# The output projection of a gated streaming-encoder block: seven products of halves in place of eight

## The chip, the cores and the metric

The kernel runs on one core of a Trainium2 chip. The metric is the device time of one execution in microseconds (us); the figure for a kernel is the median of its runs. A profile is one execution of its own, with its own time. PE is the matrix engine (TensorE), DVE VectorE, ACT ScalarE, POOL GpSimd, SP the engine that issues most of the DMAs.

## The reference, cut to what matters

One layer for 2048 tokens of width 1024, all in f32. The normalised input goes through one wide projection; branch A is banded attention, branch B ("ret") retention with a per-head norm; each branch is gated and projected back to width 1024; the two are mixed, projected once more, added to the input and normalised:

```python
branch_a = jnp.einsum('bsf,fd->bsd', o_a * jax.nn.silu(g_a), w_out_attn[l])
branch_r = jnp.einsum('bsf,fd->bsd', o_r * jax.nn.silu(g_r), w_out_ret[l])
mixed = jax.nn.sigmoid(m_a) * branch_a + jax.nn.sigmoid(m_r) * branch_r
x = x + jnp.einsum('bsd,de->bse', mixed, w_out[l]).astype(x.dtype)
...
return rms_norm(x, final_gain)
```

The change is in the line with `w_out`: a product of (2048 x 1024) by (1024 x 1024), and in how its operands are made.

## The kernel before, in words

**Products.** Every f32 matrix is kept as a high part (a cast to fp32r, on ACT) and a low part (source minus high part, on DVE or POOL). A "product" multiplies a stationary block of 512 x 128 by a moving block of 512 x 512: four slices `k` of 128, each with three matmuls of 128x512 (high by high, high by low, low by high), so 12 matmuls (`Chunk.matmuls`). The moving block lies in one of seven resident slots `R[0]` to `R[6]`, each with a high and a low tile. The stationary block is made by `make`: one ACT cast (L296) and one subtraction (L297).

**Jobs and steps.** The work on PE is one list of products, `seq`, in the order of the jobs: `p0`, `g0`, `p1`, `g1` (the wide projection), `ba0`, `ba1` (branch A's output), `br0`, `br1` (branch B's output), `out`. A job has chunks, a chunk has products. `dense()` walks the list; a product takes four steps, and `later(n, f)` runs `f` n steps on. `prime(at + ahead + 1)` with `AHEAD = 3` makes the stationary block of a product three products before PE comes to it.

**Two kinds of chunks.** `Plain` chunks (`ba`, `br`, `out`) multiply halves the ordinary way: for 256 output columns or tokens, two column halves `c`, two row halves `i` and two inner halves `j`, so eight products a chunk. `Strassen` chunks (`p`, `g`) form sums of halves and need seven: `SUMS_OF` gives four sums t1 to t4 of the streamed operand, made on POOL; the resident operand needs the quarter blocks A11, A12, A22 and four sums, in slots as `PRODUCTS` numbers them; `Strassen.product` combines the seven results with one ACT copy (`u2`) and five DVE additions, and calls `epilogue` four times. `ORDERS` are the orders in which the seven are done. The products' results lie in the PSUM banks "x", "y", "v", "z", "w", all from the pool `ACC` (4 banks); in the last phase another pool, `TR` (4 banks), stands open.

**The last phase** (`mrg`) holds the end of `g1`, the branch projections and `out`. There `strict[0]` is False: ACT, DVE and POOL instructions may be ordered by the framework rather than by the program; PE and the SP queue stay in program order. Row blocks of branch outputs are loaded into slots by `fill_ya`, `fill_yr` and `finish_yr`, at places given by `RYA` and `RYR`. All these small 128x512 buffers come from one pool `E` of 23 (`E_MRG`). `out` streams the mixed rows (`raw_out`, two loads of 512 KB a chunk, SP queue, three buffers) as stationary blocks; its four moving blocks are the quarters of `w_out`, loaded, cast and subtracted into slots 0, 2, 3, 4 by `fill_wo` (L1130) from hooks in `br1`. In `br`, each output half needs two operand loads (`gr`, `ta`), one DVE operation (L1124), one POOL addition (L1125) and a store.

**The output's epilogue** (`ep_out`, L1156). `before_out` loads 128x512 of x (`xr`) and of the final gain (`fg`). When a pair of products is done, DVE forms xr = 0.25 ps + xr (L1161), ACT squares it with a row sum (L1166), POOL multiplies by the gain (L1167). When both halves of a 128-token row are there, DVE computes the reciprocal root in tiny 128x1 operations (L1172, then `rsqrt`, L196 to L204), and the halves are scaled, one on ACT (L1175), one on DVE (L1174), and stored six steps later. The last row's first half is stored from ACT's queue.

Of the kernel before, what the change touches and what calls it, by code (L numbers as in the profile page):

```python
# [21 lines left out]
P = 128  # L22
# [23 lines left out]
ORDERS["f"] = LAST = (0, 3, 1, 2, 4, 5, 6)  # L46
AHEAD = 3
# [23 lines left out]
def hybrid_kernel(  # L71
# [196 lines left out]
    class Chunk:  # L268
# [42 lines left out]
        def bank(self, name):  # L311
            if name not in self.ps:
                self.ps[name] = ACC(f"ps_{self.job.name}_{self.c}_{name}")
            return self.ps[name]
# [13 lines left out]
    class Strassen(Chunk):  # L328
        def sum(self, dst, one, two, ring=None):
            b = self.b  # L330
            if dst in b:
                return
            name = f"{dst}_{self.job.name}_{self.c}"
            t = wp.tile([P, 4, P], F32, tag="t", bufs=SUMS, name=name) if ring is None else \
                ring(name).rearrange("p (k c) -> p k c", k=4)
            b[dst] = self.shaped(t)
            pool.tensor_tensor(b[dst], b[one], b[two], ALU.subtract)

# [75 lines left out]
    class Job:  # L414
        def __init__(self, name, n, stream, epilogue, lo_pool=(), kh=2, resident=None, before=None, front=0):
# [10 lines left out]
            if name == "p1":  # L426
                self.orders[:2] = "first", "second"
            seq = [(c, k) for c in range(front, n) for k in (per if resident else ORDERS[self.orders[c]])]
# [22 lines left out]
    def dense(jobs):  # L451
# [14 lines left out]
        sooner[at - 9], sooner[at - 6] = (one, [0]), (one, [1])  # L466
        for at, (job, ch, n) in enumerate(seq):
# [9 lines left out]
            while starts and starts[0] <= at + job.lead:  # L477
                _, ch2, n2 = seq[starts.pop(0)]
                ch2.before(n2)
            for _ in ch.product(n):  # L480
# [649 lines left out]
    def fill_wo(i, j, m):  # L1130
        def fetch(k):
            a = E(f"wo_{i}_{j}_{k}")
            row = (4 * j + k) * P
            dma(a, w_out[0, row:row + P, 512 * i:512 * i + 512])
            later(10, lambda: act.copy(R[m][0][:, k, :], a))
            later(12, lambda: dve.tensor_tensor(R[m][1][:, k, :], a, r32(R[m][0][:, k, :]), ALU.subtract))

        for k in range(4):
            later(1 + 2 * k, lambda k=k: fetch(k))
# [16 lines left out]
    def ep_out(c, i, j, src, got):  # L1156

        t = 2 * c + j
        xr, fg = got

        dve.scalar_tensor_tensor(xr, src, 0.25, xr, ALU.mult, ALU.add)  # L1161
        if t not in rows_out:
            rows_out[t] = ({}, small.tile([P, 2], F32, tag="fs", bufs=4, name=f"fs_{t}"))
        halves_, fs = rows_out[t]
        junk = E(f"jk_{t}_{i}", BF16)
        act.activation(junk, xr, AF.Square, scale=DM ** -0.5, accum_out=fs[:, i:i + 1])  # L1166
        pool.tensor_tensor(fg, xr, fg, ALU.mult)  # L1167
        halves_[i] = fg
        if len(halves_) < 2:
            return  # L1170
        ft, fr, tm, hv = (small.tile([P, 1], F32, tag=f"f{n}", bufs=2, name=f"f{n}_{t}") for n in range(4))
        dve.scalar_tensor_tensor(ft, fs[:, 0:1], NORM_EPS, fs[:, 1:2], ALU.add, ALU.add)  # L1172
        rsqrt(ft, fr, tm, hv)
        dve.tensor_scalar(halves_[1], halves_[1], fr, None, ALU.mult)  # L1174
        act.mul(halves_[0], halves_[0], fr)  # L1175
        for f in range(2):
            dst = out[0, t * P:(t + 1) * P, 512 * f:512 * f + 512]
            if t == SEQ // P - 1 and not f:
                act.dma_start(dst, halves_[f])
            else:  # L1180
                put(6, dst, halves_[f])
# [444 lines left out]
    RYA = [{(0, 0): 0, (1, 0): 4}, {(0, 0): 6, (1, 0): 1}]  # L1626
    RYR = [{(0, 0): 5, (0, 1): 3, (1, 0): 2, (1, 1): 0}, {(0, 0): 4, (0, 1): 6, (1, 0): 1, (1, 1): 5}]
    RWO = {(0, 0): 0, (0, 1): 2, (1, 0): 3, (1, 1): 4}
# [6 lines left out]
    jobs.append(Job("out", 8, mx_stream, ep_out, resident=RWO, before=before_out))  # L1635
# [14 lines left out]
    for i in range(2):  # L1650
        hook("ba0", 1 + i, 0, lambda i=i: fill_ya(1, i, RYA[1][i, 0]))
        hook("br1", 1 + i, 0, lambda i=i: fill_wo(i, 1 - i, RWO[i, 1 - i]))
    hook("br1", 0, 0, lambda: fill_wo(0, 0, RWO[0, 0]))
    hook("br1", 3, 4, lambda: fill_wo(1, 1, RWO[1, 1]))

# [146 lines left out]
```

## Time and profile before

| what | value |
|---|---|
| median of 3 runs | 1987.76 us (1986.89 to 1991.05) |
| profiled execution, its own time | 1993.2 us |
| its span, first to last instruction | 1991.4 us |
| mean granted TensorE clock | 0.996 |
| PE busy | 1926.9 us (97%) |
| DVE, ACT, POOL busy | 1353.9 (68%), 911.1 (46%), 898.8 us (45%) |
| DMA | 434.85 MB, mean 218 GB/s |

Busy shares are means over stages that differ: what a change in `out` is worth is read from the last 175 us of the span alone.

### The profile page before, as it was taken

Reading aid. Unit: us, or ns where it says so; the run is one execution under the profiler, and the core shown is the slowest. Engines: PE = TensorE matmul, PEld = TensorE weight load, DVE = VectorE, ACT = ScalarE, POOL = GpSimd, SP = SyncE. Lnnn points to the kernel's source line nnn. Section 1 sums busy time; section 2 is a strip of 40 time slices with the busy share of each in tenths; the row PEclk is TensorE's granted clock in tenths of the full one; section 3 lists DMA queues with packets and bytes.
Section 4 is the critical chain, followed back from the end, with each engine's and each line's share of the span. In section 5 each row is a group of like instructions: output and inputs, shape, how many; then the busy total and the mean of one; then the engine's idle time right before and its main releaser. Section 6 shows DMA issues by size and latency. Waiting matters only on the chain.

```text
span 1991.4 us, 30303 instructions
## 1 busy us (share of the span) xinstructions
PE 1926.9 (97%) x9712; PEld 1604.3 (81%) x9712; DVE 1353.9 (68%) x2585; ACT 911.1 (46%) x1835; POOL 898.8 (45%) x735
## 2 busy tenths in 40 slices
PE   6899999999999999999999999999999999999998
PEld 4777778888888877778787888888888878888886
DVE  7887878677766658888887677765566655544554
ACT  6454454566654545443333555554455221222332
POOL 2343544555546665544544444454675114422222
PEclk9999999999999999999999999999999999999999
DMA  4576695756549987676675645554989999976564
GB/s 148 162 258 198 217 309 197 211 153 181 159 135 276 276 248 258 192 242 195 193 247 177 185 148 177 155 147 141 281 268 294 319 334 338 326 251 213 187 200 138
DMA packets 335054, 434.85 MB, mean 218 GB/s; under 512 B 30040, under 2 KB 194544, under 8 KB 334896
## 3 DMA queue, kind: packets, MB, share of 16 engines
q1 hardware_dynamic: 277744, 377.07, 59.6%
q10 hardware_dynamic: 57152, 55.85, 9.3%
q8 instruction: 78, 1.28, 0.3%
q14 instruction: 80, 0.66, 0.1%
HBM read 288.21 MB, written 144.60 MB: 217 GB/s over the span
## 4 chain that ended last, share of the span: by engine, by line
PE 50%; DVE 7%; DMA 4%; issue 3%; ACT 1%; POOL 1%; SPq 0%; DVEq 0%; POOLq 0%; ACTq 0%
PE ps_g_z L140 4%; PE ps_g_x L140 3%; PE ps_p_z L140 3%; PE po L140 2%; PE ps_p_x L140 2%; PE wide L140 2%; PE o L140 2%; PE ps_g_v L140 2%; PE ps_g_y L140 2%; PE ps_g_w L140 2%; PE tp L140 1%; PE ps_p_w L140 1%; PE ps_p_y L140 1%; DMA raw_ba<-in_w_out_attn_dram 1%; PE ps_p_v L140 1%
## 5 line engine op out<-in xcount | busy, mean ns | idle before, releaser
L140 POOL TENSOR_SCALAR pr<-pr,rsum 128x640 f32<-128x640 f32 (+4 forms) x128 | 96.5, 754 | 225.4 <-DVE ptl L140 105.4
L140 PE MATMUL ps_g_z<-r,wh_g 128*128 128x512 f32 x448 | 144.0, 403 | 4.2 <-DVE c_g L140 4.2
L140 PE MATMUL ps_p_z<-r,wh_p 128*128 128x512 f32 x448 | 141.5, 397 | 5.4 <-DVE c_p L140 2.8
L140 PE MATMUL ps_p_x<-r,wh_p 128*128 128x512 f32 x448 | 142.0, 398 | 1.4 <-ACT u_p L140 1.4
L140 PE MATMUL ps_g_x<-r,wh_g 128*128 128x512 f32 x448 | 142.5, 399 | 0.7 <-ACT u_g L140 0.7
L140 DVE CUSTOM_DVE_ANT_0 pr<-wide,bt 128x640 f32<-128x640 f32 (+4 forms) x128 | 94.3, 737 | 71.2 <-PE wide L140 63.8
L140 POOL TENSOR_TENSOR t_p<-raw_p,t_p 128x512 f32<-128x512 f32 x50 | 74.8, 1497 | 146.9 <-DVE wl_p L140 134.1
L140 ACT ACTIVATE pr<-pr,mn 128x640 f32<-128x640 f32 (+4 forms) x128 | 98.0, 766 | 85.0 <-DVE mn L140 85.0
L140 DVE TENSOR_TENSOR ptl<-tp,pth 128x384 fp32r<-128x384 f32 x168 | 95.9, 573 | 40.9 <-ACT pth L140 40.5
L140 ACT CAST pth<-tp 128x384 fp32r<-128x384 f32 x168 | 84.8, 516 | 70.1 <-PE tp L140 66.1
L140 POOL TENSOR_TENSOR sl<-sm,sh 128x512 fp32r<-128x512 f32 x64 | 88.0, 1376 | 61.5 <-ACT sh L140 25.5
L140 DVE TENSOR_TENSOR wl_p<-t_p,wh_p 128x512 fp32r<-128x512 f32 x112 | 105.1, 939 | 2.0 <-ACT wh_p L140 2.0
L1167 POOL TENSOR_TENSOR fg<-xr,fg 128x512 f32<-128x512 f32 x32 | 44.4, 1387 | 128.3 <-DVE xr L1161 100.5
L140 DVE TENSOR_TENSOR sm<-sr,dm 128x512 f32<-128x512 f32 x64 | 44.1, 689 | 82.7 <-DMA dm<-in_dmask_dram 35.2
L140 PEld LDWEIGHTS ps_p_z<-r,wh_p 128*128 128x128 f32 x448 | 81.7, 188 | 22.9 <-issue 5.5
L140 PEld LDWEIGHTS ps_p_x<-r,wh_p 128*128 128x128 f32 x448 | 83.7, 190 | 19.9 <-ACT u_p L140 2.2
L140 PE MATMUL wide<-ka,qa 128*128 128x512 f32 (+2 forms) x448 | 94.5, 327 | 2.3 <-DVE mn L140 2.3
L1125 POOL TENSOR_TENSOR gr<-gr,ta 128x512 f32<-128x512 f32 x32 | 47.7, 1492 | 105.0 <-DVE gr L1124 89.8
L140 POOL TENSOR_TENSOR wl_g<-t_g,wh_g 128x512 fp32r<-128x512 f32 x56 | 75.2, 1342 | 40.5 <-ACT wh_g L140 31.4
L140 PEld LDWEIGHTS tp<-ident,pr 128*128 128x128 f32 x560 | 71.2, 140 | 27.2 <-POOL pr L140 2.2
L140 PE MATMUL po<-pth,va 128*128 128x256 f32 x336 | 93.0, 297 | 0.0
L140 ACT CAST wh_p<-t_p 128x512 fp32r<-128x512 f32 x112 | 69.2, 619 | 49.5 <-PE ps_p_z L140 22.1
(1187 smaller groups left out, 5969.2 us busy)
## 6 DMA issues: line engine op xcount, KB each, us to landing
raw_g<-in_w_in_dram ACTq DMA_DIRECT2D x56, 512.0 KB, 5.4
raw_p<-in_w_in_dram ACTq DMA_DIRECT2D x50, 512.0 KB, 6.1
qa<-qas SPq DMA_DIRECT2D x128, 128.0 KB, 3.0
qr<-qrs SPq DMA_DIRECT2D x128, 128.0 KB, 4.2
vr<-vrs SPq DMA_DIRECT2D x64, 256.0 KB, 5.6
ka<-kas SPq DMA_DIRECT2D x40, 256.0 KB, 3.6
va<-vas SPq DMA_DIRECT2D x40, 256.0 KB, 3.0
kds<-kdt_k SPq DMA_DIRECT2D x32, 256.0 KB, 4.5
```

The source lines that it names most:

```text
L140: return tc.keep_in_program_order(op(*a, **k))
L1125: pool.tensor_tensor(g, g, ta, ALU.add)
L1167: pool.tensor_tensor(fg, xr, fg, ALU.mult)
```

## The change

`out` becomes a job of `Strassen` chunks: seven products a chunk, eight chunks. The seven moving operands are three quarters of `w_out` (A11, A12, A22) and four sums. `fill_wo(k)` loads all four quarters of one slice k in one go (four points in `br1`), makes the sums S3 and S2 on DVE and S4 and S1 on POOL, places A11, A12 and S1 in slots 0, 1 and 3 at once, and keeps S2, S3, A22 and S4 in `E` tiles; `place_wo(m)` writes them into slots 4, 5, 2 and 6 right after the products 4, 5, 6 and 7 of `br1`'s last chunk, which are the last readers of these slots. So that the slots come free in that order, `RYA` and `RYR` put the rows of the branches elsewhere. Chunk 0 of `out` takes the order "s", the last "l", the others "o". The results "z" and "w" of `out` take their banks from `TR`. Operands of the epilogue are loaded two products ahead of a chunk, four pairs over ten steps; the mixed rows are now loaded from ACT's queue, as for all `Strassen` jobs. The root is taken for both rows of a chunk together, except in the last chunk, and there the scaling is on ACT for all four tiles.

```diff
@@ -44 +44 @@
 ORDERS = {"p": (0, 4, 1, 2, 3, 5, 6), "g": (0, 1, 3, 2, 4, 5, 6)}
 FRONT = (0, 3, 5, 1, 2, 4, 6)
 ORDERS["f"] = LAST = (0, 3, 1, 2, 4, 5, 6)
+ORDERS["s"], ORDERS["o"], ORDERS["l"] = (0, 3, 4, 1, 2, 5, 6), (0, 4, 1, 2, 3, 5, 6), (0, 4, 1, 2, 5, 6, 3)
 AHEAD = 3
 PARTS = 8
 RAWS = 3
@@ -310 +312 @@
         def bank(self, name):
             if name not in self.ps:
-                self.ps[name] = ACC(f"ps_{self.job.name}_{self.c}_{name}")
+                two_pools = self.job.name == "out" and name in ("z", "w")
+                self.ps[name] = (TR if two_pools else ACC)(f"ps_{self.job.name}_{self.c}_{name}")
             return self.ps[name]
@@ -335 +338 @@
                 ring(name).rearrange("p (k c) -> p k c", k=4)
             b[dst] = self.shaped(t)
             pool.tensor_tensor(b[dst], b[one], b[two], ALU.subtract)
+        def before(self):
+            def load(q):
+                self.got[q] = self.job.before(self.c, *q)
+            last = self.job.orders[self.c] == "l"
+            for k, q in enumerate(((1, 1), (1, 0), (0, 1), (0, 0)) if last else ((0, 0), (1, 1), (1, 0), (0, 1))):
+                later(1 + 3 * k, lambda q=q: load(q))
         def sums(self, n):
             if self.b is None and self.raw:
@@ -425 +437 @@
                 self.orders[-1] = "f"
             if name == "p1":
                 self.orders[:2] = "first", "second"
+            if name == "out":
+                self.orders[0], self.orders[-1] = "s", "l"
             seq = [(c, k) for c in range(front, n) for k in (per if resident else ORDERS[self.orders[c]])]
             if front:
@@ -464 +478 @@
         two_.raw, three.raw = [], []
         at = begins[one]
         sooner[at - 9], sooner[at - 6] = (one, [0]), (one, [1])
+        first_out = jobs[-1].chunks[0]
+        at = begins[first_out]
+        for lead in RAW_LEADS:
+            sooner.pop(at - lead)
+        sooner[at - 6], sooner[at - 4] = (first_out, [0]), (first_out, [1])
+        operands = {begins[ch] - 2: ch for ch in begins if ch.job.before}
         for at, (job, ch, n) in enumerate(seq):
             free[0] = job.name[0] == "g"
             count[ch] = count.get(ch, 0) + 1
@@ -477 +498 @@
             while starts and starts[0] <= at + job.lead:
                 _, ch2, n2 = seq[starts.pop(0)]
                 ch2.before(n2)
+            if at in operands:
+                operands[at].before()
             for _ in ch.product(n):
                 yield True
                 free[0] = job.name[0] == "g"
@@ -1127 +1150 @@
         return epilogue
-    def fill_wo(i, j, m):
-        def fetch(k):
-            a = E(f"wo_{i}_{j}_{k}")
+    wo = {}
+    def fill_wo(k):
+        a = {}
+        for i, j in ((0, 0), (1, 0), (1, 1), (0, 1)):
+            a[i, j] = E(f"wo_{i}_{j}_{k}")
             row = (4 * j + k) * P
-            dma(a, w_out[0, row:row + P, 512 * i:512 * i + 512])
-            later(10, lambda: act.copy(R[m][0][:, k, :], a))
-            later(12, lambda: dve.tensor_tensor(R[m][1][:, k, :], a, r32(R[m][0][:, k, :]), ALU.subtract))
+            dma(a[i, j], w_out[0, row:row + P, 512 * i:512 * i + 512])
+        s2, s3, s4 = (E(f"ws{n}_{k}") for n in (2, 3, 4))
+        wo[4, k], wo[5, k], wo[2, k], wo[6, k] = s2, s3, a[1, 1], s4
+        def place(m, t, eng):
+            later(1, lambda: act.copy(R[m][0][:, k, :], t))
+            later(3, lambda: eng.tensor_tensor(R[m][1][:, k, :], t, r32(R[m][0][:, k, :]), ALU.subtract))
+        def sums():
+            dve.tensor_tensor(s3, a[1, 0], a[0, 0], ALU.subtract)
+            place(0, a[0, 0], pool)
+            dve.tensor_tensor(s2, s3, a[1, 1], ALU.add)
+        def rest():
+            pool.tensor_tensor(s4, a[0, 1], s2, ALU.subtract)
+            place(1, a[0, 1], dve)
+            pool.tensor_tensor(a[1, 0], a[1, 0], a[1, 1], ALU.add)
+            place(3, a[1, 0], dve)
+        later(10, sums)
+        later(13, rest)
+    def place_wo(m):
         for k in range(4):
-            later(1 + 2 * k, lambda k=k: fetch(k))
+            def low(k=k):
+                eng = pool if k == 2 else dve
+                eng.tensor_tensor(R[m][1][:, k, :], wo[m, k], r32(R[m][0][:, k, :]), ALU.subtract)
+            later(1 + k, lambda k=k: act.copy(R[m][0][:, k, :], wo[m, k]))
+            later(2 + k, low)
     def mx_stream(c, j):
         b, u = c // 2, c % 2
@@ -1153 +1204 @@
         )
         return xr, fg
-    def ep_out(c, i, j, src, got):
+    def ep_out(c, i, j, src, ps):
         t = 2 * c + j
-        xr, fg = got
+        xr, fg = jobs[-1].chunks[c].got.pop((i, j))
         dve.scalar_tensor_tensor(xr, src, 0.25, xr, ALU.mult, ALU.add)
-        if t not in rows_out:
-            rows_out[t] = ({}, small.tile([P, 2], F32, tag="fs", bufs=4, name=f"fs_{t}"))
-        halves_, fs = rows_out[t]
+        if c not in rows_out:
+            rows_out[c] = ({}, small.tile([P, 2, 2], F32, tag="fs", bufs=3, name=f"fs_{c}"))
+        tiles, fs = rows_out[c]
         junk = E(f"jk_{t}_{i}", BF16)
-        act.activation(junk, xr, AF.Square, scale=DM ** -0.5, accum_out=fs[:, i:i + 1])
+        act.activation(junk, xr, AF.Square, scale=DM ** -0.5, accum_out=fs[:, j, i:i + 1])
         pool.tensor_tensor(fg, xr, fg, ALU.mult)
-        halves_[i] = fg
-        if len(halves_) < 2:
+        tiles[j, i] = fg
+        last = c == SEQ // T - 1
+        js = [j] if last and {(j, 0), (j, 1)} <= set(tiles) else [0, 1] if not last and len(tiles) == 4 else []
+        if not js:
             return
-        ft, fr, tm, hv = (small.tile([P, 1], F32, tag=f"f{n}", bufs=2, name=f"f{n}_{t}") for n in range(4))
-        dve.scalar_tensor_tensor(ft, fs[:, 0:1], NORM_EPS, fs[:, 1:2], ALU.add, ALU.add)
+        n = len(js)
+        ft, fr, tm, hv = (small.tile([P, n], F32, tag=f"f{k}_{n}", bufs=2, name=f"f{k}_{t}") for k in range(4))
+        dve.scalar_tensor_tensor(ft, fs[:, js[0]:js[-1] + 1, 0], NORM_EPS, fs[:, js[0]:js[-1] + 1, 1], ALU.add, ALU.add)
         rsqrt(ft, fr, tm, hv)
-        dve.tensor_scalar(halves_[1], halves_[1], fr, None, ALU.mult)
-        act.mul(halves_[0], halves_[0], fr)
-        for f in range(2):
-            dst = out[0, t * P:(t + 1) * P, 512 * f:512 * f + 512]
-            if t == SEQ // P - 1 and not f:
-                act.dma_start(dst, halves_[f])
-            else:
-                put(6, dst, halves_[f])
+        for k, j in enumerate(js):
+            t = 2 * c + j
+            for f in range(2):
+                if f and last:
+                    dve.tensor_scalar(tiles[j, f], tiles[j, f], fr[:, k:k + 1], None, ALU.mult)
+                else:
+                    act.mul(tiles[j, f], tiles[j, f], fr[:, k:k + 1])
+                dst = out[0, t * P:(t + 1) * P, 512 * f:512 * f + 512]
+                if t == SEQ // P - 2 and not f:
+                    act.dma_start(dst, tiles[j, f])
+                else:
+                    put(6, dst, tiles[j, f])
     def attention(s, sbp, ps_wide):
@@ -1623 +1682 @@
         projection("g1", 1, GATES, (2, 5)),
     ]
-    RYA = [{(0, 0): 0, (1, 0): 4}, {(0, 0): 6, (1, 0): 1}]
-    RYR = [{(0, 0): 5, (0, 1): 3, (1, 0): 2, (1, 1): 0}, {(0, 0): 4, (0, 1): 6, (1, 0): 1, (1, 1): 5}]
-    RWO = {(0, 0): 0, (0, 1): 2, (1, 0): 3, (1, 1): 4}
+    RYA = [{(0, 0): 0, (1, 0): 4}, {(0, 0): 5, (1, 0): 2}]
+    RYR = [{(0, 0): 6, (0, 1): 1, (1, 0): 3, (1, 1): 0}, {(0, 0): 4, (0, 1): 5, (1, 0): 2, (1, 1): 6}]
     for s in range(2):
         jobs.append(Job(f"ba{s}", 4, w_stream(w_out_attn, [T * c for c in range(4)], 1), ep_ba(s),
                         kh=1, resident=RYA[s], before=before_ba(s)))
     for s in range(2):
         jobs.append(Job(f"br{s}", 4, w_stream(w_out_ret, [T * c for c in range(4)]), ep_br(s),
                         resident=RYR[s], before=before_br(s)))
-    jobs.append(Job("out", 8, mx_stream, ep_out, resident=RWO, before=before_out))
+    jobs.append(Job("out", 8, mx_stream, ep_out, (2, 5), before=before_out))
     end, at = {}, 0
     for j in jobs:
         at += j.size
@@ -1649 +1707 @@
         hook("g1", 13, 6, lambda j=j: later(66 * j, lambda: fill_yr(j, RYR[0][0, j])))
     for i in range(2):
         hook("ba0", 1 + i, 0, lambda i=i: fill_ya(1, i, RYA[1][i, 0]))
-        hook("br1", 1 + i, 0, lambda i=i: fill_wo(i, 1 - i, RWO[i, 1 - i]))
-    hook("br1", 0, 0, lambda: fill_wo(0, 0, RWO[0, 0]))
-    hook("br1", 3, 4, lambda: fill_wo(1, 1, RWO[1, 1]))
+    for k in range(4):
+        hook("br1", *divmod(1 + 6 * k, 8), lambda k=k: fill_wo(k))
+    for n, m in ((4, 4), (5, 5), (6, 2), (7, 6)):
+        hook("br1", 3, n, lambda m=m: place_wo(m))
     stream = [dense(jobs)]
     seq.extend((job, ch, n) for job in jobs for ch, n in job.seq)
```

## Rows read from the trace of the kernel before

**Rows 1.** The page, parts 1 and 2: busy time; granted clock in 40 slices.
```profile
PE 1926.9 (97%) x9712; PEld 1604.3 (81%) x9712; DVE 1353.9 (68%) x2585; ACT 911.1 (46%) x1835; POOL 898.8 (45%) x735
...
PEclk9999999999999999999999999999999999999999
```
**Rows 2.** Busy time by stretch: `out`, then `br1` (PE, PEld, DVE, ACT, POOL, clock, DMA).
```profile
1809.26:1983.36 174.10, 174.08 (x769) 143.80 (x767) 84.99 (x228) 51.06 (x107) 44.80 (x32) 1.00 0.57 183
1722.22:1809.26 87.04, 87.04 (x386) 72.07 (x385) 37.90 (x51) 20.51 (x34) 25.96 (x19) 1.00 0.80 264
```
**Rows 3.** The chain that ended last, from 1800 us: start, duration, what.
```profile
1809.26 5.44 PE ps_out_(0, 0)_19976 L140 x24
...
1890.86 5.44 PE ps_out_(1, 1)_20690 L140 x24
...
1977.90 5.45 PE ps_out_(1, 1)_21435 L140 x24
...
1983.38 0.70 DVE xr L1161
...
1987.30 0.72 ACT fg L1175
```
**Rows 4.** Who waited for whom on PE, 840 to 1080 us (`p1`): total, times, longest.
```profile
PE ps_p_z L140 <- DVE c_p L140: 1.2, 2, 0.8
PE ps_p_y L140 <- DVE wl_p L140: 0.4, 1, 0.4
```
**Rows 5.** The tile u_p on ACT: who waited for it (us, times).
```profile
  PE ps_p_x L140: 1.4, 2
```
**Rows 6.** DVE's timeline, 1972 to 1984 us: the last row but one.
```profile
1972.50 0.69 DVE L1161 SCALAR_TENSOR_TENSOR xr<-ps_out_(0, 1)_21353,xr 128x512 f32<-128x512 f32 x1 [4.75 <-PE ps_out_(0, 1)_21353 L140]
...
1976.46 0.49 DVE L1174 TENSOR_SCALAR fg<-fg,f 128x512 f32<-128x512 f32 x1
```
**Rows 7.** DVE's timeline, 1886 to 1892 us.
```profile
1886.23 0.69 DVE L297 TENSOR_TENSOR wl_out_(0, 0)_20661<-raw_out,wh_out_(0, 0)_20660 128x512 fp32r<-128x512 f32 x1 [5.52 <-ACT wh_out_(0, 0)_20660 L296]
1886.84 0.68 DVE L1161 SCALAR_TENSOR_TENSOR xr<-ps_out_(0, 1)_20597,xr 128x512 f32<-128x512 f32 x1
...
1891.26 0.49 DVE L1174 TENSOR_SCALAR fg<-fg,f 128x512 f32<-128x512 f32 x1
1891.66 0.68 DVE L1161 SCALAR_TENSOR_TENSOR xr<-ps_out_(1, 0)_20647,xr 128x512 f32<-128x512 f32 x1
```
**Rows 8.** DVE's timeline, 1842 to 1846 us.
```profile
1843.09 1.80 DVE L297 TENSOR_TENSOR wl_out_(0, 1)_20304<-raw_out,wh_out_(0, 1)_20303 128x512 fp32r<-128x512 f32 x1 [0.18 <-ACT wh_out_(0, 1)_20303 L296]
1844.81 0.15 DVE L1172 SCALAR_TENSOR_TENSOR f<-fs 128x1 f32<-128x1 f32 x1
```
**Rows 9.** Groups by line, `out`, DVE: count, busy us, mean ns, idle before.
```profile
L1172 DVE SCALAR_TENSOR_TENSOR f<-fs 128x1 f32<-128x1 f32 x16 | 10.9, 679 | 3.2 <-ACT jk L1166 3.2
```
**Rows 10.** Groups by line, POOL: `out`; `p1`; `br1`; and the whole span (the page).
```profile
L1167 POOL TENSOR_TENSOR fg<-xr,fg 128x512 f32<-128x512 f32 x32 | 44.4, 1387 | 128.3 <-DVE xr L1161 100.5 <-DMA xr<-in_x_dram 13.8 <-ACT wh_out_(0, 1)_20683 L296 5.6
...
L140 POOL TENSOR_TENSOR t_p<-raw_p 128x512 f32<-128x512 f32 x10 | 16.2, 1620 | 8.7 <-DVE wl_p L140 8.1 <-POOL t_p L140 0.7
...
L1125 POOL TENSOR_TENSOR gr<-gr,ta 128x512 f32<-128x512 f32 x16 | 22.9, 1434 | 57.8 <-DVE gr L1124 55.6 <-DMA ta<-tas 2.1
...
L140 POOL TENSOR_TENSOR wl_g<-t_g,wh_g 128x512 fp32r<-128x512 f32 x56 | 75.2, 1342 | 40.5 <-ACT wh_g L140 31.4
```
**Rows 11.** ACT's timeline where `out` begins: casts back to back.
```profile
1808.98 0.61 ACT L296 CAST wh_out_(1, 0)_19993<-raw_out 128x512 fp32r<-128x512 f32 x1
1809.50 0.62 ACT L296 CAST wh_out_(1, 1)_20020<-raw_out 128x512 fp32r<-128x512 f32 x1
```
**Rows 12.** DMA issues, 1722 to 1992 us: count, KB each, median us to landing.
```profile
raw_out<-mxs SPq DMA_DIRECT2D x16, 512.0 KB, 5.1
...
wo<-in_w_out_dram SPq DMA_DIRECT2D x16, 256.0 KB, 4.5
```
**Rows 13.** PE's waits from 1560 us to the end: the longest of three.
```profile
PE ps_ba_(0, 0)_18298 L140 <- ACT wh_ba_(0, 0)_18218 L296: 1.0, 1, 1.0
```

## The prediction

> **What bounds the kernel now.** The page comes first: PE is busy for 97% of the span and its clock is granted almost in full from end to end [rows 1]. That is a mean over stages, so the stretch the change touches is read next. In the busy time by stretch, `out` lasts 174.10 us and PE is busy for 174.08 of them; in `br1` it is 87.04 of 87.04, while DVE is at 49% and 44%, POOL at 26% and 30% [rows 2]. PE waits for nobody in the last 260 us. Third, the chain of waits, to see that no other work ends last: it runs through `out` on PE alone, 32 blocks of 24 matmuls of 5.44 us each, and only then has a tail: xr at 1983.38, the scaling at 1987.30, the end of the span at 1991.4 [rows 3]. A block is two products, so a product costs 2.72 us, and a product less is 2.72 us less, as long as the next stationary block, the slot and the PSUM bank are there in time.
>
> **The change part by part.** The sum is made against the profiled execution, 1993.2 us (1991.4 of span and 1.8 around it); the median shown, 1987.76, is 5.4 lower, and the difference is carried over to it.
>
> *Products.* 64 become 56, all of 12 matmuls of the same shape: 8 x 2.72 = **-21.8**.
>
> *Order "s" of chunk 0.* Product 3 follows product 0 at once and adds to the same bank "x", which ACT must first have copied into u2. In `p0` and `p1` PE waited for that copy twice, 1.4 us in all [rows 5]: **+0.7**. Between 0 and 2.8: ACT's casts come 0.52 us apart [rows 11], and the last `place_wo` puts four of them ahead of the copy.
>
> *The tail.* Before, the last row's two halves are two blocks apart from the row ahead. With "l", the other row ends with the last product but one, 2.72 us before the end. Then DVE has u2's addition, xr, the root and the scaling. A DVE operation follows another 0.61 us later [rows 7], so that xr starts at -2.10 from PE's end; from xr to the scaling it is 1976.46 - 1972.50 = 3.96 us [rows 6], and 0.40 on DVE is free [rows 7]: at +2.26 in place of +0.02. That DVE finishes a root before an xr that has come free is what rows 7 show: the block ended at 1890.86 [rows 3], its xr started at 1891.66. **+2.2**; 0 if the xr is slipped in between. The rest of the tail is as before.
>
> *Operands, steady.* A chunk has on DVE five low parts, five additions and four xr, 14 x 0.61 = 8.5, and a root of 13 operations in place of two of ten: the ten take 1.98 from the first to the scaling, three more about 0.2 each, so 2.6; together 11.1 of 19.04 us. POOL has four sums (1.62 at most by `p1`), two low parts (1.34) and four gains (1.39): 14.7 of 19.04, 77% where it was 26% [rows 10]. ACT, at 51.06 us in eight chunks [rows 2], 6.4 each, gets three more casts, a copy and two more scalings, at most 6 x 0.72 (the scaling's own time, rows 3): 10.7. So no engine is full, and a stationary block is begun three products, 8.2 us, ahead. What of it shows on PE is taken from `p1`, the same kind of chunk, where PE waited for DVE 1.2 + 0.4 us in 240 [rows 4]: for 152.3 us **+1.0**; `out` itself had none, and it can be no gain, as there is no wait to lose.
>
> *The transition.* Four `place_wo` put 16 casts and 16 low parts (12 on DVE, 4 on POOL) into `br1`'s last products. Each slot is written right after its last reader and read again six products, 16.3 us, later; casts need 4 x 0.52, low parts 3 x 0.61 a slot, so nothing is late: 0. The upper end is in the rivals. The load into these slots in the kernel before had the same shape and no wait.
>
> *fill_wo.* 16 loads of 256 KB stay 16, in four bursts instead of spread ones; SP puts them out one behind the other, and a burst lands in some 5 us [rows 12]. Behind it stand `gr`, `ta` and the next raws, used four or more products (10.9 us) later: 0. The eight sums on DVE and eight on POOL fall where these two are busy 44% and 30%: 0. They hold `E` tiles, four a slice, 16 at the end and 19 at the fullest moment of 23: if it were over 23, SP would stand until `place_wo(4)`, nine products or 24.5 us.
>
> *Queues and places.* 16 loads of the mixed rows leave SP for ACT, 5.1 us each to land [rows 12], issued two chunks' blocks ahead: 0. SP then only has operands and stores. The new places in `RYA`/`RYR` name slots that are free at the same hooks: 0; the ends are the waits that `ba` has, the longest of the three 1.0 us [rows 13], either way.
>
> Sum: -21.8 + 0.7 + 2.2 + 1.0 = **-17.9**: 1975.3 for a profiled execution, **1969.9 us** for the median.
>
> *DVE beside POOL.* A low part that runs beside a POOL operation took 1.80 us where it takes 0.69, and the root's first operation, 0.15 us alone, took 0.68 on average [rows 7 to 9]. So an operation with two SBUF inputs waits for POOL, and POOL becomes three times as busy. Waits before, per chunk: two roots of 0.53 and at most one low part of 1.11, so 2.2 over 18 such operations, 0.12 each. Times 77/26 it is 0.36 each, for 15 (five low parts, ten in the root) 5.4: DVE comes to 16.5 of 19.04 and stays under PE. That is why I keep +1.0.
>
> The Trainium skill, SBUF — State Buffer, section "SBUF: two separate sides", says that VectorE and GpSimd share one pair of ports by an exclusive lock held for the whole instruction, and that the loser blocks fully. By that rule a VectorE operation of this kind may lose a whole GpSimd operation each time, which speaks against moving sums to GpSimd; the rows above agree with it for single operations, and no row shows a root beside a GpSimd queue without gaps. By it the sum would be that of rivals 2 and 3.
>
> **The rivals.**
>
> 1. *The transition is late.* Operations that exclude one another, ahead of chunk 0's fourth stationary block: three `place_wo` (3 x 0.61 + 1.3 each, 9.4), three sums and t4 (1.3 each, 5.2), two `gr` additions (1.43, 2.9) [rows 10], four low parts (2.4): 19.9 us, where 16.3 are there from the first `place_wo` on. PE waits 3.6 in place of 1.0: 1972.5. For it: the exclusion. Against it: the same slot fill of 4 + 4 before left PE without a wait [rows 2]. 12%.
>
> 2. *DVE becomes the bound, by a little.* At a mean wait of 0.53 for its 15 operations DVE needs 11.1 + 8 = 19.04 and PE starts to wait; at 0.61 a chunk takes 20.25, 8 x 1.21 = 9.7 more: -21.8 + 2.9 + 9.7 = -9.2, **1978.6**. For it: POOL's queue has few gaps. Against it: in `p1` a fuller DVE cost PE next to nothing [rows 4]. 9%.
>
> 3. *The same, all the way: slower.* The gain is gone when a chunk takes 21.4 us, a mean wait of 0.69. At the longest waits, 1.11 for a low part and about 0.83 for the root's first, mean 0.97, a chunk takes 25.7 us: (25.7 - 21.76) x 8 + 2.9 = +34, **2022**. Against it: the present mean wait is 0.12, a sixth of what is needed. 3%.
>
> **How the numbers follow.** Forecast 72%, rivals 12, 9 and 3%, something unforeseen 4%. A measurement can tell about 0.2%, 4 us, from no change. Faster by more: forecast, rival 1, rival 2 and part of the rest, 0.94; the same 0.03; slower 0.03. The forecast's own ends: all costs at nothing gives -21.8, 1966.0, and with the lowest of the runs shown (0.9 under the median) 1965; with all at their upper ends (2.8, 2.2, 3.6) -13.2, 1974.6. Rival 1 lies inside; the range is drawn into rival 2 up to 1977, which leaves out most of rival 2, 3 and the unforeseen.
>
> **What would show it.** PE with 96 matmuls fewer (9616); blocks of `out` 2.72 us apart with `out` some 153 to 155 us long; one wait of PE for the u2 copy of chunk 0; in the tail, the last xr some 2 us after PE's end. POOL over 70% in `out`, the root longer than 2.6 us, low parts often over 1 us. Wrong would be the forecast if PE waits in each chunk for low parts or for c22 and u3 (rivals 2, 3), or at chunk 0's fourth product (rival 1), or if SP stands in `br1` before a load of `w_out`.

## The result: slower by 0.4%, and the profile after

The changed kernel takes 1993.29 us in the median of 21 runs (1990.30 to 2000.12), the kernel before 1987.11 in as many (1979.27 to 1993.94): a ratio of 1.0036, 95% interval 1.0027 to 1.0045. The forecast was 1969.9 us, with a range of 1965 to 1977. The profiled execution after took 1991.35 us, 1989.6 of it span.

First the page of the changed kernel, busy time; it answers to [rows 1].

```profile
PE 1913.1 (96%) x9616; PEld 1586.9 (80%) x9616; DVE 1422.6 (72%) x2582; ACT 936.9 (47%) x1893; POOL 994.7 (50%) x799
```

The 96 matmuls are gone (9712 to 9616), and PE is busy for 13.8 us less, but not for 21.8. By stretch, `br1` and then `out` (columns as in [rows 2]):

```profile
1714.54:1801.58 87.04, 87.04 (x385) 72.07 (x385) 49.17 (x55) 23.66 (x43) 50.56 (x35) 1.00 0.78 261
1801.58:1977.10 175.52, 159.42 (x661) 125.94 (x661) 135.65 (x208) 73.02 (x153) 114.91 (x79) 0.97 0.56 180
```

`br1` has taken on the sums and the filling of the slots (DVE 37.90 to 49.17, POOL 25.96 to 50.56) without a gap on PE. The loss is all in `out`: 56 products should last 152.3 us, and they take more than the 174.10 of the 64 before: the second window ends 2.7 us ahead of PE's last matmul, and from `out`'s first matmul to that end it is 178.4. Below, "the stage" is the time from `out`'s first matmul to the end of the span: 182.1 us before, 188.2 after, 6.1 more; the medians differ by 6.2. The stages ahead of `out` shift by some us from one execution to the next in either kernel (it began at 1809.26 before, at 1801.4 after), so single kernels are compared by their stage.

The busy time over the stage after shows what the 188.2 us are: 162.32 busy, so 25.9 without a matmul, of which 9.8 are the tail behind the last product and 16.1 are waits. The 162.32 are themselves 10.0 more than 152.3.

```profile
1801.40:1989.60 188.20, 162.32 (x673) 127.99 (x671) 143.26 (x233) 76.09 (x160) 117.46 (x81) 0.96 0.54 174
```

The waits of PE in it (total, times, longest):

```profile
PE ps_out_w L142 <- ACT wh_out L298: 6.0, 4, 1.6
PE ps_out_w L142 <- POOL wl_out L299: 3.7, 6, 0.6
PE ps_out_z L142 <- DVE c_out L394: 3.6, 2, 3.2
PE ps_out_v L142 <- POOL wl_out L299: 1.0, 1, 1.0
PE ps_out_x L142 <- ACT u_out L381: 1.0, 1, 1.0
PE ps_out_y L142 <- DVE wl_out L299: 0.7, 1, 0.7
```

The product "w" waits in nearly every chunk, first for ACT's cast of its stationary block (t4), then for POOL's low part of it. The 10 us of longer matmuls go in part with the clock: its granted mean fell to 0.93, 0.89 and 0.83 in three of the ten-us stretches between 1855 and 1935 us (part of each at 1.2 in place of 2.4 GHz). In the first and the last of these PE had stood for 2.1 us; it stood for 2.2 from 1835 to 1845, too, at the full clock. Another part lies around the waits: chunk 0, at the full clock, lasts 22.9 us, 3.9 more than seven products, and only 2.7 of it are waits. The last of the three stretches:

```profile
1925.00:1935.00 10.00, 7.95 (x27) 6.08 (x27) 7.16 (x10) 4.98 (x12) 6.03 (x5) 0.83 1.00 311
```

Now one chunk, read back from such a gap on PE. PE's timeline (start, duration, tile, in brackets the idle time and its releaser):

```profile
1902.97 0.39 PE L142 MATMUL ps_out_x<-r,wl_out 128*128 128x512 f32 x1
1904.79 0.73 PE L142 MATMUL ps_out_w<-r,wh_out 128*128 128x512 f32 x2 [1.43 <-ACT wh_out L298]
1906.13 0.50 PE L142 MATMUL ps_out_w<-r,wl_out 128*128 128x512 f32 x1 [0.61 <-POOL wl_out L299]
```

ACT's timeline shows why the cast was late. It was idle for 5.24 us with the four scalings at the head of its queue, which waited for DVE's root (in the first seven chunks ACT scales all four tiles; in the last, DVE takes two); the casts for "w" and for the chunk's last product stand behind them:

```profile
1895.85 0.58 ACT L381 COPY u_out<-ps_out_x 128x512 f32<-128x512 f32 x1
1901.67 2.56 ACT L1235 ACTIVATE fg<-fg,f 128x512 f32<-128x512 f32 x4 [5.24 <-DVE f L211]
1904.13 0.60 ACT L298 CAST wh_out<-t_out 128x512 fp32r<-128x512 f32 x1
1904.64 0.61 ACT L298 CAST wh_out<-raw_out 128x512 fp32r<-128x512 f32 x1
```

DVE's timeline shows the root, from L1227 to the last L211:

```profile
1895.47 0.38 DVE L1227 SCALAR_TENSOR_TENSOR f<-fs 128x2 f32<-128x2 f32 x1 [0.79 <-ACT jk L1217]
1895.88 1.23 DVE L198 TENSOR_SCALAR f<-f 128x2 int32<-128x2 int32 x1
...
1897.35 1.13 DVE L209 TENSOR_TENSOR f<-f,f 128x2 f32<-128x2 f32 x1
1898.51 1.21 DVE L210 TENSOR_TENSOR f<-f,f 128x2 f32<-128x2 f32 x1
1899.65 0.68 DVE L299 TENSOR_TENSOR wl_out<-raw_out,wh_out 128x512 fp32r<-128x512 f32 x1
1900.25 0.15 DVE L211 SCALAR_TENSOR_TENSOR f<-f,f 128x2 f32<-128x2 f32 x1
1900.43 0.16 DVE L209 TENSOR_TENSOR f<-f,f 128x2 f32<-128x2 f32 x1
1900.63 0.16 DVE L210 TENSOR_TENSOR f<-f,f 128x2 f32<-128x2 f32 x1
...
1901.41 0.16 DVE L211 SCALAR_TENSOR_TENSOR f<-f,f 128x2 f32<-128x2 f32 x1
```

It lasts 6.1 us, 0.7 of it a low part that stands in between; its operations alone were put at 2.6. Three operations on two numbers per partition take 1.13 to 1.23 us each; L209 and L210 take 0.16 later in the same root. POOL's timeline beside it:

```profile
1895.79 1.29 POOL L299 TENSOR_TENSOR wl_out<-t_out,wh_out 128x512 fp32r<-128x512 f32 x1
1897.16 1.30 POOL L340 TENSOR_TENSOR t_out<-raw_out,t_out 128x512 f32<-128x512 f32 x1
1898.42 1.29 POOL L1218 TENSOR_TENSOR fg<-xr,fg 128x512 f32<-128x512 f32 x1
```

POOL's three operations end at 1897.08, 1898.46 and 1899.71, DVE's three at 1897.11, 1898.48 and 1899.72. Each small operation ends with the POOL operation beside it. When POOL's queue is empty, at 1899.7, the root runs at its own pace. The Trainium skill, SBUF — State Buffer, section "SBUF: two separate sides", describes an exclusive lock on the ports that the two engines share, held for a whole instruction. These rows agree with it, operation by operation, for L209 and L210, which have two inputs in SBUF; L198 has one, and the last section comes back to it.

### The profile page after: what moved, and what is told of

It is laid out like the page before. It is cut to its first block, busy times and chain, and to the rows that moved or that the text cites. A ratio compares the mean times of both kernels' runs of the same rounds, so it can differ in the third digit from the quotient of the medians.

```text
span 1989.6 us, 30295 instructions
## 1 busy us (share of the span) xinstructions
PE 1913.1 (96%) x9616; PEld 1586.9 (80%) x9616; DVE 1422.6 (72%) x2582; ACT 936.9 (47%) x1893; POOL 994.7 (50%) x799
## 4 chain that ended last, share of the span: by engine, by line
PE 73%; DVE 14%; DMA 5%; issue 4%; ACT 3%; POOL 1%; SPq 1%; ACTq 0%; DVEq 0%; POOLq 0%
PE ps_g_z L142 6%; PE ps_g_x L142 6%; PE ps_p_z L142 6%; PE ps_p_x L142 5%; PE po L142 4%; PE wide L142 4%; PE ps_g_y L142 3%; PE ps_g_v L142 3%; PE ps_g_w L142 3%; PE tp L142 3%; PE o L142 3%; PE ps_p_y L142 2%; PE ps_p_w L142 2%; PE ps_p_v L142 2%; DVE u_p L142 2%
## 5 line engine op out<-in xcount | busy, mean ns | idle before, releaser
L142 PE MATMUL tp<-ident,pr 128*128 128x128 f32 x560 | 89.0, 273 | 2.9 <-POOL pr L142 1.6
L142 PEld LDWEIGHTS wide<-ka,qa 128*128 128x128 f32 x448 | 75.3, 188 | 19.2 <-DVE mn L142 7.7
```

The lines of the kernel that those rows point to most:

```text
L142: return tc.keep_in_program_order(op(*a, **k))
```

## The experiments

Three theories stood at the start. *The queue*: the scalings' place in ACT's in-order queue holds the casts. *The port*: DVE and POOL, taking turns, stretch the low parts and the root. *DVE as the bound*: it has too much to do. A fourth blamed the stores on SyncE's queue. The table has the stage, and per chunk, from the third to the seventh copy of u2: the spacing of the copies, DVE's busy time, DVE's waits for casts and squares, ACT's wait for the root. The time is that of a single execution; the kernel before took 1987.18, 1986.85 and 1985.72 us beside the first four, the next three and the last four.

| kernel | stage us | spacing | DVE busy | DVE waits | ACT for root | time us |
|---|---|---|---|---|---|---|
| changed kernel | 188.2 | 21.76 | 16.76 | 4.73 | 5.25 | 1991.35 |
| e1_no_root | 170.3 | 19.41 | 13.13 | 1.6 | none | 1976.82 |
| e2_no_scaling | 172.8 | 19.91 | 18.02 | 1.5 | none | 1980.46 |
| e3_scalings_behind_casts | 183.1 | 21.61 | 18.47 | 1.2 | none | 1987.45 |
| e4_rows_loaded_sooner | 193.1 | 23.03 | 18.00 | 4.65 | 6.83 | 2000.37 |
| e5_scaling_on_vector | 185.5 | 21.68 | 19.68 | 1.5 | none | 1990.19 |
| e6_no_gain | 170.1 | 19.97 | 14.96 | 4.85 | 4.45 | 1970.09 |
| e7_stores_later | 189.7 | 21.77 | 16.75 | 4.4 | 5.22 | 1996.79 |
| e8_root_in_psum | 166.8 | 18.60 | 13.52 | 3.1 | 1.88 | 1971.24 |
| e9_gain_and_root_in_one | 175.0 | 20.65 | 18.73 | 1.7 | none | 1981.03 |
| e10_gain_loaded_once | 173.3 | 20.12 | 18.20 | 1.7 | none | 1978.17 |
| e11_both | 167.1 | 19.01 | 16.91 | 1.0 | none | 1977.35 |

**One link taken out.** e1:

```diff
-        rsqrt(ft, fr, tm, hv)
+        if last:
+            rsqrt(ft, fr, tm, hv)
+        else:
+            fr = ft
```

> Left out: the reciprocal root of the rows' mean squares in the first seven of the eight chunks of the output (its eleven operations after the first sum), so that their scalings take the sum itself. The changed kernel takes 21.7 us a chunk in the output's stage (from one chunk's scalings to the next) and 188.0 us from the stage's first product to the end. The theory of the queue (the four scalings stand in ScalarE's queue ahead of the casts for the chunk's last two products, and wait for the root): the wait shrinks by the root's 6 us, the chunk comes down to 19.0 to 19.8, and the stage to 169 to 176. The theory of VectorE as the bound (it has no time left): the chunk falls by about the root's time, also to 19 or less. The theory of the shared port (the low parts on GpSimd and VectorE stretch one another): the low parts and their stretch stay, 20.5 to 21.7 a chunk, 180 to 188.

17.9 us of the stage came back. The spacing is 19.41, inside the range of the queue and a little above the 19 of DVE as the bound; the port, put there on the low parts, fell short. The root is a link of the chain. e2 takes out the next one, ACT's `act.mul` in all chunks but the last:

```diff
-                else:
+                elif last:
                     act.mul(tiles[j, f], tiles[j, f], fr[:, k:k + 1])
```

> Left out: the four scalings by the root in the first seven of the eight chunks (their stores put out the unscaled tiles); the root itself stays. The theory of the queue: nothing is left in ScalarE's queue that waits for the root, so the casts run on time: 19.0 to 19.5 us a chunk in place of 21.7, and 168 to 174 us from the stage's first product to the end in place of 188.0. VectorE as the bound: its operations are untouched, 21.2 to 21.7 a chunk and 184 to 188. The shared port: the root and the low parts still stretch one another, 21 to 21.7 and 183 to 188. The theory of the stores (on SyncE's queue they wait for the scalings and hold the next loads of x): 20.5 to 21.3, since the stores wait for the products alone.

19.91 in place of 19.0 to 19.5, the stage inside the queue's range. DVE did as much as before and more (18.02 a chunk): that it was full in the changed kernel, by its work alone, is ruled out. The scalings' wait is a link too, and the root got no shorter by its removal: it lasts 8.2 us here, as POOL's queue no longer runs dry beside it. e3 keeps all of the work and moves only that wait:

```diff
-    pe, act, dve, pool = Ordered(nc.tensor), Sometimes(nc.scalar), Sometimes(nc.vector), Sometimes(nc.gpsimd)
+    pe, act, dve, pool = Ordered(nc.tensor), Kept(nc.scalar), Sometimes(nc.vector), Sometimes(nc.gpsimd)
...
-                    act.mul(tiles[j, f], tiles[j, f], fr[:, k:k + 1])
...
+                scaled() if last else later(17, scaled)
```

(`Kept` keeps ACT's written order within `out`; `scaled` holds the scaling and the store.)

> Nothing is left out. In the output's stage ScalarE's instructions keep the order in which the program writes them, and the scalings of a chunk are written seventeen steps later, behind the casts for the next chunk's last two products. The theory of the queue: by then the root is long done, nothing waits for it, 19.0 to 19.6 us a chunk in place of 21.7, and 169 to 176 us from the stage's first product to the end in place of 188.0. VectorE as the bound, or the shared port: as the changed kernel, 21.2 to 21.7 and 184 to 188. What may spoil it for the first theory: the squares, which wait for VectorE, now stand ahead of casts in the written order too.

Here the queue's theory missed. The casts no longer wait for the root, and DVE waits 1.2 us a chunk in place of 4.73, but it is busy 18.47 in place of 16.76, and the spacing falls by 0.15. Only 5.1 us of the stage came back; in the written order the squares, which wait for DVE, hold the casts (ACT waited 9.75 a chunk for them). e5 leaves the order of the casts alone, and gives DVE the scalings:

```diff
-                if f and last:
+                if f or not last:
                     dve.tensor_scalar(tiles[j, f], tiles[j, f], fr[:, k:k + 1], None, ALU.mult)
```

> Nothing is left out. The four scalings of each of the first seven chunks run on VectorE behind the root, in place of ScalarE; the root, the low parts, the gain products on GpSimd and the stores stay. The theory of the queue: nothing in ScalarE's queue waits for the root, so 19.3 to 20.2 us a chunk in place of 21.7 (without the scalings it was 19.91), and 170 to 175 us from the stage's first product to the end in place of 188.2. VectorE as the bound: it takes on four operations of some 0.5 us, 22.5 us or more a chunk, 193 or more. The stores (SyncE's stores wait for the scalings and hold the loads): as the changed kernel, since the scalings end at about the same time, 21 to 22 and 184 to 190.

185.5: the queue's theory, by itself, falls. ACT waits for no root, and yet the spacing is 21.68. The theory of the bound, with 193 or more, missed as well; only the range of the stores holds 185.5, and e7 below rules these out. PE's waits from 1840 to 1950 us, and DVE's group of one root line:

```profile
PE ps_out_z L142 <- DVE c_out L394: 7.9, 4, 2.4
...
L210 DVE TENSOR_TENSOR f<-f,f 128x2 f32<-128x2 f32 x17 | 11.9, 701 | 0.6
```

DVE is now the bound, at 19.68 busy of 21.68. Its four scalings account for 1.9 of the 2.9 that it gained; the rest is a root that meets POOL more often (8.2 us long; L210: 701 ns in the mean, 512 in the changed kernel, 0.16 us alone).

**POOL taken away from the root.** e6 leaves out POOL's gain products in seven chunks:

```diff
-        pool.tensor_tensor(fg, xr, fg, ALU.mult)
-        tiles[j, i] = fg
+        if last:
+            pool.tensor_tensor(fg, xr, fg, ALU.mult)
+        tiles[j, i] = fg if last else xr
```

> Left out: the products with the final gain on GpSimd in the first seven chunks; ScalarE scales the rows themselves, in the same place of its queue. GpSimd then runs little while VectorE makes the root. If the root's 6 us are mostly waits for the port that GpSimd holds, it falls to about 2.6, the scalings come 3.5 sooner, and the theory of the queue gives 19.0 to 19.8 us a chunk and 168 to 175 from the stage's first product to the end, in place of 21.7 and 188.2. If the root is long for another reason (VectorE's own order), it stays at 5 or more and the chunk at 21 or more. VectorE as the bound by its work alone: 21 or more, too.

```profile
L209 DVE TENSOR_TENSOR f<-f,f 128x2 f32<-128x2 f32 x18 | 7.7, 430 | 0.6
L198 DVE TENSOR_SCALAR f<-f 128x2 int32<-128x2 int32 x6 | 7.4, 1234 | 0.2
...
L210 DVE TENSOR_TENSOR f<-f,f 128x2 f32<-128x2 f32 x18 | 2.9, 162 | 0.6
```

The stage is inside the range, the spacing 0.17 above it, but not in the way that was expected. L210 is back at 162 ns; L198 and the first L209 still wait for POOL's low part and sums, and the root lasts 5.1 to 5.7 us, not 2.6. ACT's queue keeps the order of the changed kernel: the scalings still stand ahead of the casts and wait 4.45 us a chunk, and DVE still waits 4.85. What fell is DVE's busy time, by 1.80, and with it the spacing, by 1.79. So the place in the queue, with DVE less slowed, leaves the chunk 0.9 above the 19.04 of seven products. But this run takes away POOL's work as well as the waits. e8 was meant to take away the waits alone, and of the root only: its sum `ft` and its iterate `fr` are moved to PSUM.

```diff
+        end = fr
+        if not last:
+            tiny = TR(f"tiny_{c}")
+            ft, fr = tiny[:, 0:2], tiny[:, 2:4]
...
-        rsqrt(ft, fr, tm, hv)
+        rsqrt(ft, fr, tm, hv, None if last else end)
+        fr = end
```

(In `rsqrt` the shift writes `y`, and the last of the three steps writes `end`, in SBUF, for ACT.)

> Nothing is left out, and every engine keeps its instructions and their order. In the first seven chunks the sum and the iterate of the root lie in PSUM, so that of its thirteen operations no one but the first and one of each triple's inputs touches SBUF for a second operand. The theory of the port (the root is 6 us long because its operations wait for the SBUF port that GpSimd's gain products and low parts hold): the root falls to 3 us or less, the scalings come 3 sooner, VectorE is busy 13.5 to 14.5 us a chunk in place of 16.8, and the chunk takes 19.0 to 20.2 in place of 21.76, the stage 169 to 176 in place of 188.2. If the root's length is VectorE's own latency or order: still 5 or more, and 21 or more a chunk. The theory of the queue alone (the position of the scalings, whatever the port does): the wait for the root stays above 4 us a chunk and the chunk above 21.

The stage falls by 21.4 us, to less than either side expected. The root in DVE's timeline:

```profile
1887.21 0.39 DVE L1232 SCALAR_TENSOR_TENSOR tiny<-fs 128x2 f32<-128x2 f32 x1 [0.79 <-ACT jk L1218]
1887.63 0.17 DVE L199 TENSOR_SCALAR tiny<-tiny 128x2 int32<-128x2 int32 x1
...
1888.14 1.23 DVE L300 TENSOR_TENSOR wl_out<-raw_out,wh_out 128x512 fp32r<-128x512 f32 x1
1889.29 0.15 DVE L210 TENSOR_TENSOR f<-tiny,f 128x2 f32<-128x2 f32 x1
...
1890.83 0.16 DVE L212 SCALAR_TENSOR_TENSOR f<-f,tiny 128x2 f32<-128x2 f32 x1
```

3.8 us where 3 or less were expected; 1.23 of them are a low part that the order puts in between and that still waits for POOL, and without it the root is at 2.6. No operation of the root behind the first is over 0.17 us. The busy time of 1840 to 1952 us, and PE's waits in the whole stage:

```profile
1840.00:1952.00 112.00, 112.00 (x496) 92.77 (x495) 81.95 (x164) 57.90 (x120) 81.26 (x57) 1.00 0.66 218
...
PE ps_out_x L142 <- ACT u_out L382: 1.5, 1, 1.5
PE ps_out_v L142 <- POOL wl_out L300: 1.1, 1, 1.1
PE ps_out_y L142 <- DVE wl_out L300: 0.9, 1, 0.9
```

PE has no gap for 112 us and its clock is granted in full; what it waits for lies in chunk 0. (The spacing of 18.60 is that of ACT's copies, which catch up on a late chunk 0; PE's own chunk is 7 x 2.72 = 19.04 us.) The page counts the same instructions on every engine as in the changed kernel, and POOL's busy time a chunk is the same 14.3 us.

Their order is not the same, though the expectation says so. In this phase the framework orders ACT's instructions, and in e8 one of the two casts, that of t4 for "w", stands ahead of the four scalings; in the changed kernel and in e6 both stand behind them. (e1 has another order again: its scalings stand ahead of the copy of u2.) ACT's timeline of e8:

```profile
1887.59 0.58 ACT L382 COPY u_out<-ps_out_x 128x512 f32<-128x512 f32 x1
1888.86 0.62 ACT L299 CAST wh_out<-t_out 128x512 fp32r<-128x512 f32 x1 [0.69 <-POOL wl_out L300]
1891.03 2.56 ACT L1241 ACTIVATE fg<-fg,f 128x512 f32<-128x512 f32 x4 [1.55 <-DVE f L212]
1893.49 0.60 ACT L299 CAST wh_out<-raw_out 128x512 fp32r<-128x512 f32 x1
```

So the 21.4 us are those of a root without waits and of a cast in a better place. e10 and e11 below are the cleaner pair: ACT and POOL have the same order in both, only the root moves to PSUM (and one low part by two places in DVE's queue), and the root falls from 6.0 us or more to 3.7, the chunk from 20.12 to 19.01, the stage by 6.2. That the root's waits for POOL cost time is shown by it. How much of the 21.4 is theirs is not; an estimate from e8's rows, with all else as it is there, makes the cast's place small. Behind the scalings it would have ended at 1894.1 here and its low part at 1895.4, and PE took them from 1896.99 on; over the six chunks from the second to the seventh the low part would have been late once, by 0.3 us. e8 with the old order was not run.

**Stores and loads.** e7 and e4:

```diff
-                    put(6, dst, tiles[j, f])
+                    put(6 if last else 16, dst, tiles[j, f])
```

> Nothing is left out. The stores of a chunk's four tiles are issued sixteen steps (four products) behind the scalings in place of six, so that SyncE's queue never stands at a store that waits for a scaling. The theory of the stores: 20.5 us a chunk or less in place of 21.7, and 180 or less from the stage's first product to the end in place of 188.2. The theory of the queue, VectorE as the bound and the port: 21.3 to 22 and 185 to 191.

```diff
-        operands = {begins[ch] - 2: ch for ch in begins if ch.job.before}
+        operands = {begins[ch] - 4: ch for ch in begins if ch.job.before}
```

> Nothing is left out. The rows of x and of the gain of a chunk are loaded from four products ahead of it in place of two. The theory of the stores and loads (SyncE's stores wait for the scalings and the next chunk's rows stand behind them, which the chain shows with 3.2 us in two chunks): 20.5 us a chunk or less in place of 21.7, 180 us or less from the stage's first product to the end in place of 188.0. The theory of the queue, VectorE as the bound and the shared port: no change, 21.4 to 21.9 and 186 to 190.

Stores that never stand in the way change nothing (21.77). Loads two products sooner made it worse by 4.9 us, which no theory expected: ACT's wait for the root grew to 6.83 a chunk, the root itself to 7.2 us in the mean, and POOL waited 1.7 for loads of the gain. Why is open.

**Another way out.** In e9 one DVE operation, row times root times gain, replaces POOL's gain product and ACT's scaling; in e10 the gain is also loaded once; in e11 the root is also in PSUM.

```diff
...
+                    xr, fg = tiles[j, f]
+                    dve.scalar_tensor_tensor(xr, xr, fr[:, k:k + 1], fg, ALU.mult, ALU.mult)
```

> Nothing is left out. In the first seven chunks one operation of VectorE behind the root (row times root times gain) takes the place of GpSimd's gain product and of ScalarE's scaling. VectorE takes on four operations of 0.69 us (2.8 a chunk) and loses most of its waits for the port, GpSimd loses 5.6 us, ScalarE 2.6. The account of VectorE (busy with port waits, plus what it waits for the casts): 14.96 busy without the gain products, plus 2.8, plus some 1.5 of waits, is 19.2, so TensorE sets the pace: 19.1 to 19.9 us a chunk in place of 21.76, 168 to 175 from the stage's first product to the end in place of 188.2. VectorE as the bound by its work alone (more operations, slower): 21.7 or more, as with the scalings on VectorE, 185 or more.

> Nothing is left out. As the run before this one, and the gain is loaded once for the first seven chunks, in place of once for each tile (26 loads of 256 KB fewer). If the loads of the gain cost something (they stand in SyncE's queue and fill the DMA engines): 0.2 to 1 us a chunk less than the run before. If not: the same within 0.3 us a chunk and 3 us in the stage.

> Nothing is left out. The root's sum and iterate in PSUM, the gain and the root in one operation of VectorE, the gain loaded once. If the port is what is left of VectorE's loss: 19.05 to 19.4 us a chunk, TensorE without gaps, 167 to 172 from the stage's first product to the end, 1968 to 1975 for the whole. If the root's waits do not matter once GpSimd is quiet: the same as the run before this one within 0.2 us a chunk.

e9's stage is at the upper end and its spacing, 20.65, outside: DVE was busy 18.73 where 17.8 were worked out, since POOL's sums and low parts still meet the root (L209 to L211 at 420 to 504 ns). e10 gains 0.5 a chunk over e9, as said. In e11 the chunk is 19.01, at the lower end of what was said, with DVE at 16.91; the total, 1977.35, misses its range because `out` began at 1808.5 us in that execution (1802.7 in e8). It is no better than e8 in the stage, with more edited, so e8 was timed:

> The kernel of e8_root_in_psum again, timed in five rounds beside the kernel before. The theory of the port: the stage of 166.8 us comes back within 2 us, 15 less than the 182.1 of the kernel before, so 1971 to 1975 as the median and a ratio to the kernel before of 0.991 to 0.994. If the single time of 1971.24 was luck in the earlier stages: 1976 to 1982, a ratio of 0.995 to 0.998. Slower than the kernel before, or no difference, would contradict the theory.

1973.70 us in the median (1969.30 to 1977.81) beside 1987.71: a ratio of 0.9923, 95% interval 0.9904 to 0.9942. The stage came back at 166.8. This version is faster than both kernels, by 0.8% and, by the medians, 1.0%.

## Why the prediction was wrong

- **Products: right.** In e8, 56 products and their three waits put PE's end 152.3 + 3.5 = 155.8 us behind the first matmul; it shows 157.0.
- **`fill_wo`, queues and places: right.** `br1` has no gap.
- **Order "s" and the transition: a little more.** The copy of u2 cost 1.0 us, inside its bounds, where 0.7 was forecast. The transition, put at 0, cost 1.7: PE waited for low parts at chunk 0's fourth and fifth products (0.7 and 1.0). That is the place that rival 1 named, at half of its size.
- **Tail: right in size, by another way.** 9.8 us from the last product to the end, where [rows 3] give 8.05: +1.8 for +2.2. The last xr was slipped into the first root, which the text had put at zero cost; but the second root had to wait for the first. That the size came out is luck.
- **"Operands, steady": this is the step that failed**, at "So no engine is full, and a stationary block is begun three products, 8.2 us, ahead", and again at "DVE comes to 16.5 of 19.04 and stays under PE. That is why I keep +1.0". It cost 23.4 us, not 1.0: 16.1 of waits and 10.0 of longer matmuls in the stage, less the 2.7 of waits in chunk 0 that stand above. DVE's sum itself was good: 16.76 measured for 16.5. What failed was to take it as a share of time in which DVE always finds its next operand. The waits were spread as a mean of 0.36 us over 15 operations. By that mean the root would have been 2.6 + 10 x 0.36 = 6.2 us long, which is about what it is, but the text added it to DVE's busy time and did not ask who stands until it ends. In truth the root meets three POOL operations in a row (a low part, a sum, the last gain product), and lasts 6.1; the scalings wait for it at the head of ACT's queue, 5.25 a chunk; the two casts behind them come that much later; DVE then stands 3.73 for casts and 1.0 for squares. 16.76 + 4.73 is 21.49 of the 21.76.
- **Lead time was counted at issue, not at the queue.** A block begun 8.2 us ahead is not ready 8.2 us ahead when its cast stands behind an instruction that waits for another engine. ACT was reckoned at 10.7 of 19.04 and is at 9.5: its busy time was never the matter.
- **Rivals 2 and 3 had the cause but not the way.** They put the loss of the whole gain at a mean wait of 0.69. Measured, with all that DVE lost put on those 15, it is (16.76 - 11.1) / 15 = 0.38, and the gain was already gone. The rule of the Trainium skill that was weighed there gave the right sign; the text noted that no row showed a root beside a full POOL queue, and then priced it by the mean all the same.

How the two parts, the slowed root and the wait for it, share the loss is shown only roughly. DVE's busy time and its waits in the table add up to the spacing within 0.7 us in every row but e1, e3, e8 and e11, so that both lengthen the chunk. With a long root and no wait of ACT for it the chunk fell to 19.91 (e2), or not at all where DVE took on the scalings (e5); with ACT's order kept and a root shorter by 0.8 us it fell to 19.97, with less work on POOL (e6); with a root of 3.8 us and a wait of 1.88 PE has no gap for 112 us, with a cast moved (e8). What each would cost with everything else held was not separated.

## What to carry to other kernels

Where busy shares leave room, follow the loop once round by latency: from the late result, through every in-order queue in which something waits for it, to the work of the bottleneck that stands behind. Beside a GpSimd queue without gaps, expect a chain of small VectorE operations on SBUF to lose about a whole GpSimd operation for each of those that runs beside it (1.2 us here, for work of 0.16; three operations of the root in the changed kernel, five in e2 and e5), not the mean of rows where GpSimd was mostly idle. Scratch of a chain of small operations may lie in PSUM: that edit, with the order that the framework then chose, turned this change from 0.4% slower to 0.8% faster. And where a framework orders the queues, read their order again after each edit: here a change of memory on VectorE moved a cast on ScalarE.

## What was not expected of the hardware

An operation with a single SBUF input waited too: L198, a shift of 128x2 numbers, took 1.22 us in the mean of the first seven chunks, and 0.17 with both sides in PSUM. An operation with one input in PSUM and one in SBUF, on the same POOL queue, did not wait (L210: 156 ns in e8). And the low parts' waits for POOL did not hold PE by themselves: in e8 they still took 0.87 and 1.39 us in the mean, for 0.69 alone, and PE had no gap.
